# Layer 1's u and gate columns in pairs: seven half-size products for eight, on an x that is normalised before it is split

## The chip, the cores and the metric

The kernel runs on one core of a Trainium2 chip. The metric is the time of one execution in device microseconds; times shown are medians of runs, and the traces come from one profiled execution.

## The reference, cut to what matters

1,024 prompt rows and 64 sample rows (1,088 tokens, width 1,024) pass through two layers. The second one is the odd layer:

```
def _odd_layer(x, g_norm, w_in, ln_g, ln_b, w_s, b_s, w_out):
    z = _rmsnorm(x, g_norm) @ w_in                      # w_in: 1024 x 6144
    uv = jax.nn.gelu(z[..., :2 * D_C]); gate = z[..., 2 * D_C:]
    u = uv[..., :D_C]; v = _layernorm(uv[..., D_C:], ln_g, ln_b)
    # per head of 256 columns: causal 128x128 mixing of v inside each chunk of 128 rows
    y = (u * mix * jax.nn.silu(gate)) @ w_out
    return x + y, v[:, start:]
```

## The kernel before

Everything is float32 in exactness: each operand is split into a high part (type fp32r) and a low part (what is left), and a product is three matmuls, high x high, high x low, low x high, accumulated in one PSUM buffer. ScalarE copies the high part, VectorE subtracts to get the low one (`split`, L125 and the helper line L92; VectorE's operations made through helpers all bear the line L92, so its groups are told apart by their tiles).

x is held transposed, eight tiles of 128 features by 1,088 tokens, high and low. A unit (`unit`, `unit_w`, L460 to L468) makes 128 output columns for all tokens: three token pieces of 368, 352 and 368 columns (`PIECES`), and for each, eight depth tiles of three matmuls. Weights come by `wload` (512 KB each into two buffers `wr`) and `wsplit` (three buffers each of `wh`, `wl`, or a pair of the big pool for the roomy kinds); `wget` keeps two more split ahead.

The stages of the second half of the program: the fourth part of the first layer's output projection (unit after unit, each adds into x1, takes the square for the norm, and splits x1 times the norm's gain into `xh`, `xl`); `token_wide` for v (four groups of 512 columns, token rows as the stationary side, L545 to L556, evacuated through gelu with the row's norm factor `rc`, L1189, and statistics, L1190); then eight heads of 256 columns. In a head, two units give u and two give the gate, each evacuated from PSUM by a VectorE product with `rb`, the norm factor spread over partitions (L1163 to L1165); `prepare` normalises the head's v and transposes the mixing matrix; `mixed` applies it (L1274, L1279); y is split and stored to DRAM, except four of sixteen tiles that stay in SBUF for the first part of the last projection. `out_part` then adds four parts of depth 512, with operands fetched from DRAM during the part before.

The norm's per-row factors come from 18 one-column matmuls:

```
    for t in range(9):
        n = rows(t)
        mm(mp[0:n, t:t + 1], s2[:, t * P:t * P + n], one1[:, 0:1], start=True, stop=True)
```

The first layer is issued in an order written out by hand. From the fourth part of its projection on, only SyncE's queue (the loads) keeps the order of the program text; on the other engines a planner takes, of what it holds to be ready, the instruction that stands first in the text. SBUF tiles come from pools of fixed size, `ft` with 31 buffers being the large one; a tile waits until an older one has been read for the last time. PSUM has four buffers for units (`ps_mm`) and four for the rest.

Of the kernel before, what the change touches and what calls it, by code (L numbers as in the profile page):

```python
# [15 lines left out]
P = 128  # L16
D = 1024
# [4 lines left out]
T = NPR + NS  # L22
KD = D // P
# [12 lines left out]
def kernel(  # L36
# [91 lines left out]
    def wload(spec):  # L128
        kind, w2d, rws, c0 = spec
        shape = {"u": [P, 8, P], "h": [P, 4, 256], "q": [P, 2, 512], "qf": [P, 2, 512]}[kind]  # L130
# [3 lines left out]
        return raw, shape, kind == "qf"  # L134
# [37 lines left out]
    for part in (2, 3, 0, 1):  # L172
        for mg in range(4):
            plan_h(wo0, mg * 256, 4 * part, 1)
    for g in range(4):
        for q in range(4):
            wspecs.append(("q" if q % 2 == 0 else "qf", w1, 2 * q, 2048 + 512 * g))
    for h in range(8):
        for d in range(2):
            plan_u(w1, (2 * h + d) * P)  # L180
            plan_u(w1, 4096 + (2 * h + d) * P)
    PARTS1 = ([8, 9, 10, 11], [0, 1, 2, 3], [4, 5, 6, 7], [12, 13, 14, 15])
    for ks in PARTS1[:3]:
        for mg in range(4):
            plan_h(wo1, mg * 256, ks[0], 1)
# [156 lines left out]
    mcaus = cst.tile([P, P], I32, name="mcaus")  # L342
# [4 lines left out]
    bm4 = cst.tile([96, 4], F32, name="bm4")  # L347
# [4 lines left out]
    msamp = cst.tile([NS, NS], I32, name="msamp")  # L352
    mblk = cst.tile([NS, NSB], I32, name="mblk")
    scm = cst.tile([P, 512 + NS], F32, name="scm")
# [27 lines left out]
    cwt = cst.tile([P, CW, KD], F32, name="cwt")  # L382
# [4 lines left out]
    lbt = cst.tile([P, 4, KD], F32, name="lbt")  # L387
# [145 lines left out]
    def token_wide(ah, al, tail, evac):  # L533
# [5 lines left out]

        for t in range(8):  # L540
# [8 lines left out]
        ps = ps_mm("ps")  # L549
        for k in range(KD):  # L550
            wh, wl = w(k)
            if k > 0:
                mm(ps[0:NS, :], tail[:, k - 1, 0:NS], w(k - 1)[1], start=False, stop=False)
            if k == KD - 1:
                mm(ps[0:NS, :], tail[:, k, 0:NS], wl, start=False, stop=False)
            mm(ps, tail[:, k, :], wh, start=(k == 0), stop=(k == KD - 1))  # L556
        tl = th("tl", [NS, 512])
        act(out=tl, in_=ps[NS:P, :], func=AF.Copy)
        tt_op(out=tl, in0=ps[0:NS, :], in1=tl, op=ALU.add)
        evac(8, NS, tl)  # L560
# [573 lines left out]
    x1_d = dscr("x1_d", KD)  # L1134
    xh, xl = [], []
    s2 = None
    for mg in range(4):
        (wh, wl), = wget()
        for s in range(2):
            m = 2 * mg + s  # L1140
            ms = slice(s * P, (s + 1) * P)
            xm = x1[m]
            unit_w([(wh[:, k, ms], wl[:, k, ms]) for k in range(4)], bh, bl, accum(x1)(m))
            hi, lo = ft(f"gh{m}", F32R), ft(f"gl{m}", F32R)
            act(out=hi, in_=xm, func=AF.Copy, scale=col(o_nc, m))
            stt(out=lo, in0=xm, scalar=col(o_nc, m), in1=hi.bitcast(F32), op0=ALU.mult, op1=ALU.subtract)
            sq = ft("sq")
            act(out=sq, in_=xm, func=AF.Square)
            if s2 is None:
                s2 = sq  # L1150
            else:
                tt_op(out=s2, in0=s2, in1=sq, op=ALU.add)
# [245 lines left out]
```

## Time and profile before

| | |
|---|---|
| median of 3 runs | 1824.42 us (1821.47 to 1824.86) |
| the profiled execution | 1825.03 us, span 1823.2 us |
| TensorE, VectorE, ScalarE busy in the span | 1803.2, 1126.8, 682.8 us |
| mean granted TensorE clock | 0.998 of 2.4 GHz |
| moved to and from DRAM | 196.4 MB, 108 GB/s |

The span runs from the first to the last instruction; the execution's own time is 1.8 us longer. TensorE's busy time is a union of overlapping matmuls. A granted clock of 1.00 is 2.4 GHz, 0.50 is 1.2 GHz.

### The profile page before, as it was taken

The page shows a single profiled execution, that of the slowest core. Times are in us where ns is not written, and L with a number is a line of the kernel's source. Part 1 is how long each engine was busy: PE and PEld are TensorE (multiplying, and loading weights), DVE is VectorE, ACT ScalarE, POOL GpSimd, SP SyncE. Part 2 cuts the span into 40 slices and gives each one's busy share as a digit, 9 for nine tenths or more (in the row PEclk, how much of TensorE's full clock was granted, in tenths as well). Part 3 has the DMA queues.
Part 4 walks back from the last instruction along what each step waited for, and adds up shares of the span by engine and source line. Part 5 has one row for each costly group of instructions (what it writes and reads, how often), then busy time and mean ns, then how long its engine had stood idle before and what let it go on. Part 6 is the DMA issues. An engine that isn't in the chain of part 4 may idle for free.

```text
span 1823.2 us, 27162 instructions
## 1 busy us (share of the span) xinstructions
PE 1803.2 (99%) x11360; PEld 1742.8 (96%) x11360; DVE 1126.8 (62%) x1801; ACT 682.8 (37%) x1100; POOL 18.0 (1%) x50
## 2 busy tenths in 40 slices
PE   7999999999999999999999999999999999999998
PEld 6999999999999999999999888899999999999996
DVE  6468779878887878847776342244555454543434
ACT  5234442545255544645324232232323233320124
POOL 0000000000000000000000000000000000000000
PEclk9999999999999999999999999999999999999999
DMA  5112122213122212388423222334443221374501
GB/s 165 49 39 83 51 100 60 97 51 109 57 79 63 84 49 96 109 283 287 163 96 123 103 95 85 106 96 133 133 128 90 91 73 59 98 292 155 179 24 75
DMA packets 178650, 196.44 MB, mean 108 GB/s; under 512 B 7560, under 2 KB 151376, under 8 KB 178512
## 3 DMA queue, kind: packets, MB, share of 16 engines
q1 hardware_dynamic: 153256, 139.00, 24.0%
q10 hardware_dynamic: 25272, 55.71, 8.0%
q8 instruction: 89, 1.46, 0.3%
q14 instruction: 33, 0.27, 0.0%
HBM read 138.98 MB, written 56.42 MB: 107 GB/s over the span
## 4 chain that ended last, share of the span: by engine, by line
PE 98%; DVE 1%; ACT 1%; DMA 0%; issue 0%; ACTq 0%; SPq 0%; DVEq 0%
PE ps L466 23%; PE ps L468 23%; PE ps L467 23%; PE ps L547 3%; PE ps L545 3%; PE ps L546 3%; PE ps L504 2%; PE ps L505 2%; PE ps L506 2%; PE mp L1274 2%; PE ps L1354 1%; PE ps L1352 1%; PE ps L1353 1%; PE dp L777 1%; PE op L797 1%; PE op L857 1%
## 5 line engine op out<-in xcount | busy, mean ns | idle before, releaser
L466 PE MATMUL ps<-xh,wh 128*128 128x368 f32 (+1 forms) x1080 | 356.7, 330 | 0.0
L468 PE MATMUL ps<-xh,wl 128*128 128x368 f32 (+1 forms) x1080 | 352.8, 327 | 0.0
L467 PE MATMUL ps<-xl,wh 128*128 128x368 f32 (+1 forms) x1080 | 352.7, 327 | 0.0
L92 DVE SCALAR_TENSOR_TENSOR y<-ab,cwt,y 128x1024 f32<-128x1024 f32 x240 | 306.7, 1278 | 0.2
L125 ACT ACTIVATE wh<-wr 128x1024 fp32r<-128x1024 f32 x124 | 130.7, 1054 | 346.4 <-PE ps L467 248.1
L466 PE MATMUL ps<-gh,wh 128*128 128x368 f32 (+1 forms) x768 | 252.8, 329 | 0.0
L468 PE MATMUL ps<-gh,wl 128*128 128x368 f32 (+1 forms) x768 | 251.4, 327 | 0.0
L467 PE MATMUL ps<-gl,wh 128*128 128x368 f32 (+1 forms) x768 | 250.8, 327 | 0.0
L92 DVE TENSOR_TENSOR wl<-wr,wh 128x1024 fp32r<-128x1024 f32 x124 | 151.4, 1222 | 150.4 <-ACT wh L125 149.2
L466 PEld LDWEIGHTS ps<-xh,wh 128*128 128x128 f32 x1080 | 202.7, 188 | 1.3
L467 PEld LDWEIGHTS ps<-xl,wh 128*128 128x128 f32 x1080 | 202.8, 188 | 0.3
L468 PEld LDWEIGHTS ps<-xh,wl 128*128 128x128 f32 x1080 | 202.7, 188 | 0.0
L92 DVE TENSOR_TENSOR x<-ps,x 128x368 f32<-128x368 f32 x168 | 88.4, 533 | 115.4 <-PE ps L468 112.8
L466 PEld LDWEIGHTS ps<-gh,wh 128*128 128x128 f32 x768 | 144.2, 188 | 0.3
L467 PEld LDWEIGHTS ps<-gl,wh 128*128 128x128 f32 x768 | 144.2, 188 | 0.0
L468 PEld LDWEIGHTS ps<-gh,wl 128*128 128x128 f32 x768 | 144.2, 188 | 0.0
L466 PE MATMUL ps<-oh,wh 128*128 128x368 f32 (+1 forms) x384 | 127.6, 332 | 0.0
L468 PE MATMUL ps<-oh,wl 128*128 128x368 f32 (+1 forms) x384 | 125.5, 327 | 0.0
L467 PE MATMUL ps<-ol,wh 128*128 128x368 f32 (+1 forms) x384 | 125.4, 327 | 0.0
L92 DVE TENSOR_TENSOR g<-ps,rb 128x368 f32<-128x368 f32 (+1 forms) x48 | 25.7, 535 | 121.1 <-PE ps L468 121.1
L1190 DVE BATCH_NORM_STATS2 bst<-vq 128x6 f32<-128x512 f32 x32 | 22.0, 693 | 120.0 <-ACT vq L1189 120.0
L504 PE MATMUL ps<-wh,xh 128*128 128x256 f32 x256 | 72.9, 285 | 0.0
(328 smaller groups left out, 3402.5 us busy)
## 6 DMA issues: line engine op xcount, KB each, us to landing
wr<-in_w_in_ab_dram SPq DMA_DIRECT2D x56, 512.0 KB
wr<-in_w_in_c_dram SPq DMA_DIRECT2D x48, 512.0 KB
yr<-y_d SPq DMA_DIRECT2D x16, 544.0 KB
wr<-in_w_out_ab_dram SPq DMA_DIRECT2D x16, 512.0 KB
v_d<-vq ACTq DMA_DIRECT2D x16, 512.0 KB
wr<-in_w_out_c_dram SPq DMA_DIRECT2D x16, 512.0 KB
yh_d<-yh ACTq DMA_DIRECT2D x12, 544.0 KB
yl_d<-yl ACTq DMA_DIRECT2D x12, 544.0 KB
```

The lines of the kernel that those rows point to most:

```text
L92: return f(**kw)
L125: act(out=hi, in_=src, func=AF.Copy)
L466: mm(ps[:, 0:cn], wh, ah[k][:, cs], start=(k == 0), stop=False)
L467: mm(ps[:, 0:cn], wh, al[k][:, cs], start=False, stop=False)
L468: mm(ps[:, 0:cn], wl, ah[k][:, cs], start=False, stop=(k == n_k - 1))
L504: mm(ps[:, 0:256], ah[k][:, ts], wh, start=(k == 0), stop=False)
L505: mm(ps[:, 0:256], ah[k][:, ts], wl, start=False, stop=False)
L506: mm(ps[:, 0:256], al[k][:, ts], wh, start=False, stop=(k == KD - 1))
L545: mm(ps, ah[k][:, ts], wh, start=(k == 0), stop=False)
L546: mm(ps, ah[k][:, ts], wl, start=False, stop=False)
L547: mm(ps, al[k][:, ts], wh, start=False, stop=(k == KD - 1))
L1274: mm(mp[:, b * P:(b + 1) * P], vr[4 * g + b][:, ds_], wsT, start=True, stop=True)
```

## The change

- The four units of a head become two pairs: the two u units (256 columns), then the two gate units. Seen as a 2 x 2 block matrix (x halved by depth and by tokens, the weights by depth and by columns), a pair takes seven products of half depth (four tiles), half columns (128) and half tokens (544, in two pieces of 272) where plain multiplication takes eight. The blocks of sums and differences of x (`halves`) are made once, in the v part; those of the weights (`s_prep`) for each pair. Each product is added from PSUM into one or two of the four output quarters.
- x1's norm is applied to x before the split (`normed`), piece by piece; the output projection's last part runs pieces outside, units inside. The products with `rb` and the factors `rc` go, and with them the one-column matmuls.
- The nine normalisations of v per head move from VectorE to ScalarE. `mixed` multiplies u in place. All sixteen y tiles go to DRAM, in half tiles; the last projection takes them in order, its first part reloaded too.
- The small pools of the first layer are closed and new ones opened; the last v group does its sample rows first.

The diff, cut to its core:

```diff
+HT = T // 2
...
+            wspecs.append(("hf" if part == 1 and mg == 3 else "h", wo0, 4 * part, mg * 256))
     for g in range(4):
         for q in range(4):
...
+            kind = (("q", "q", "q", "qf"), ("qf", "qf", "q", "q"), ("q", "qf", "q", "qf"), ("q", "qf", "q", "q"))[g][q]
+            wspecs.append((kind, w1, 2 * q, 2048 + 512 * g))
+    PARTS1 = ([0, 1, 2, 3], [4, 5, 6, 7], [8, 9, 10, 11], [12, 13, 14, 15])
...
+    def token_wide(ah, al, tail, evac, tail_first):
...
+        if tail_first:
+            decode()
...
+    def cx(name, dt=F32):
+        return sp1.tile([P, HT], dt, tag="cx", bufs=4, name=name)
...
+    def tw(name, shape):
+        return sp1.tile(list(shape), F32, tag="tw", bufs=2, name=name)
...
+    xh = [ft(f"gh{m}", F32R) for m in range(KD)]
+    xl = [(ft if m < 5 else fu)(f"gl{m}", F32R) for m in range(KD)]
...
+    def normed(j, s2):
+        c0, cn = PIECES[j]
+        cs = slice(c0, c0 + cn)
+        mp = ps_ax("mp")
+        mm(mp[:, 0:cn], one1, s2, start=True, stop=True)
+        rb = cx("rb")[:, 0:cn]
+        act(out=rb, in_=mp[:, 0:cn], func=AF.Sqrt, scale=1.0 / D, bias=epsc)
+        nc.vector.reciprocal(out=rb, in_=rb)
+        for m in range(KD):
+            xn = cx("xn")[:, 0:cn]
+            stt(out=xn, in0=x1[m][:, cs], scalar=col(o_nc, m), in1=rb, op0=ALU.mult, op1=ALU.mult)
+            act(out=xh[m][:, cs], in_=xn, func=AF.Copy)
+            tt_op(out=xl[m][:, cs], in0=xn, in1=xh[m][:, cs].bitcast(F32), op=ALU.subtract)
+            yield
+    wq = wget(4)
+    for j, (c0, cn) in enumerate(PIECES):
+        cs = slice(c0, c0 + cn)
+        s2 = tw("s2", [P, HT])[:, 0:cn]
+        for m in range(KD):
+            wh, wl = wq[m // 2]
+            ms = slice(m % 2 * P, m % 2 * P + P)
+            ps = ps_mm("ps")
+            for k in range(4):
+                mm(ps[:, 0:cn], wh[:, k, ms], bh[k][:, cs], start=(k == 0), stop=False)
+                mm(ps[:, 0:cn], wh[:, k, ms], bl[k][:, cs], start=False, stop=False)
+                mm(ps[:, 0:cn], wl[:, k, ms], bh[k][:, cs], start=False, stop=(k == 3))
+            tt_op(out=x1[m][:, cs], in0=ps[:, 0:cn], in1=x1[m][:, cs], op=ALU.add)
+            store(out=x1_d[m][:, cs], in_=x1[m][:, cs])
+            if m == 0:
+                act(out=s2, in_=x1[m][:, cs], func=AF.Square)
             else:
+                sq = cx("sq")[:, 0:cn]
+                act(out=sq, in_=x1[m][:, cs], func=AF.Square)
                 tt_op(out=s2, in0=s2, in1=sq, op=ALU.add)
...
-
-    mp = ps_ax("mp")
-    for t in range(9):
-        n = rows(t)
-        mm(mp[0:n, t:t + 1], s2[:, t * P:t * P + n], one1[:, 0:1], start=True, stop=True)
...
+            aside()
+        side.append(normed(j, s2))
...
+    def halves(i):
+        def part(nm, k, cs):
+            t = cx(nm)
+            tt_op(out=t, in0=xh[k][:, cs].bitcast(F32), in1=xl[k][:, cs].bitcast(F32), op=ALU.add)
+            return t
+        def parted(r, t):
...
+            h, l = sums_h[r, i // 2][:, i % 2, :], sums_l[r, i // 2][:, i % 2, :]
+            act(out=h, in_=t, func=AF.Copy)
+            tt_op(out=l, in0=t, in1=h.bitcast(F32), op=ALU.subtract)
+        a21, s = part("a21", i, HI), part("a22", i + 4, HI)
+        yield
+        tt_op(out=s, in0=s, in1=a21, op=ALU.subtract)
+        parted(1, s)
+        yield
+        a11 = part("a11", i, LO)
+        tt_op(out=diff[i // 2][:, i % 2, :], in0=a11, in1=a21, op=ALU.subtract)
+        yield
+        stt(out=s, in0=s, scalar=-1.0, in1=a11, op0=ALU.mult, op1=ALU.subtract)
+        parted(2, s)
+        yield
+        a12 = part("a12", i + 4, LO)
+        stt(out=s, in0=s, scalar=-1.0, in1=a12, op0=ALU.mult, op1=ALU.subtract)
+        parted(3, s)
...
+    def s_load(c0):
+        ks = []
+        for q in range(2):
+            raw = wrp.tile([P, 4, 256], F32, tag="wr", name="wr")
+            load(out=raw, in_=w1[q * 512:(q + 1) * 512, c0:c0 + 256].rearrange("(k p) c -> p k c", p=P))
+            ks.append(raw)
+        return ks
+    def s_prep(ks, ops):
+        b11, b12 = ks[0][:, :, 0:P], ks[0][:, :, P:256]
+        b21, b22 = ks[1][:, :, 0:P], ks[1][:, :, P:256]
+        t41, t23 = tw("t41", [P, 2, 4, P]), tw("t23", [P, 2, 4, P])
+        tt_op(out=t41[:, 1], in0=b11, in1=b12, op=ALU.add)
+        tt_op(out=t23[:, 0], in0=t41[:, 1], in1=b22, op=ALU.add)
+        tt_op(out=t23[:, 1], in0=b22, in1=b12, op=ALU.add)
+        tt_op(out=t41[:, 0], in0=t23[:, 0], in1=b21, op=ALU.add)
+        for two in ((b11, t23[:, 0]), (b21, t23[:, 1]), (t41,), (b22,)):
+            wh = whp.tile([P, 2, 4, P], F32R, tag="wh", name="wh")
+            wl = whp.tile([P, 2, 4, P], F32R, tag="wl", name="wl")
+            if two[0] is t41:
+                split(wh, wl, t41)
+            else:
+                for e, src in enumerate(two):
+                    split(wh[:, e], wl[:, e], src)
+            ops.extend((wh[:, e], wl[:, e]) for e in range(1 if two[0] is b22 else 2))
+            yield
+    pairs = [c for h in range(8) for c in (256 * h, 4096 + 256 * h)]
+    sraw = []
...
+            aside(3 if g == 0 else 1)
+            if g == 0 and t == 4:
+                tl1.append(tails(xh, xl))
+            if t == 4 and g in (1, 2):
+                side.append(halves(g - 1))
+            if t == 0 and g == 3:
+                side.extend([halves(2), halves(3)])
+            if t == 2 and g == 3:
+                sraw.append(s_load(pairs[0]))
         if g == 0:
...
+            tl1 = []
+        token_wide(xh, xl, tl1, evac, g == 3)
+    aside(99)
+    tl1 = s2 = x1 = None
+    for i in range(4):
+        act(out=xh[i][:, HI], in_=diff[i // 2][:, i % 2, :], func=AF.Copy)
+        tt_op(out=xl[i][:, HI], in0=diff[i // 2][:, i % 2, :], in1=xh[i][:, HI].bitcast(F32), op=ALU.subtract)
+    diff = None
...
-            tsc(out=vr[t][0:n, :], in0=vr[t][0:n, :], scalar1=rv[0:n, t:t + 1], scalar2=nm[0:n, t:t + 1],
-                op0=ALU.mult, op1=ALU.add)
+            act(out=vr[t][0:n, :], in_=vr[t][0:n, :], func=AF.Identity, scale=rv[0:n, t:t + 1], bias=nm[0:n, t:t + 1])
...
+            us = u[:, g * 512:(g + 1) * 512]
+            tt_op(out=us, in0=us, in1=mx[:, 0:512], op=ALU.mult)
...
+    def a_(k0, cs):
+        return [(xh[k][:, cs], xl[k][:, cs]) for k in range(k0, k0 + 4)]
+    def s_(r):
+        return [(sums_h[r, i // 2][:, i % 2, :], sums_l[r, i // 2][:, i % 2, :]) for i in range(4)]
+    def pair_units(ops, d0, d1, func, after, ready):
+        xs = (a_(0, LO), s_(2), a_(4, LO), a_(0, HI), a_(4, HI), s_(1), s_(3))
+        for n, xk in enumerate(xs):
+            while len(ops) <= n:
+                after(-1)
+            wh, wl = ops[n]
+            for j in range(2):
+                ps = ps_mm("ps")[:, 0:HT // 2]
+                lo = slice(j * (HT // 2), (j + 1) * (HT // 2))
+                hi = slice(HT + lo.start, HT + lo.stop)
+                for k, (xhk, xlk) in enumerate(xk):
+                    mm(ps, wh[:, k], xhk[:, lo], start=(k == 0), stop=False)
+                    mm(ps, wh[:, k], xlk[:, lo], start=False, stop=False)
+                    mm(ps, wl[:, k], xhk[:, lo], start=False, stop=(k == 3))
+                if n == 0:
+                    act(out=d0[:, hi], in_=ps, func=AF.Copy)
+                for dst, src in (((), ((d1[:, lo], d0[:, hi]),), ((d0[:, lo], d0[:, hi]),), ((d1[:, hi], d1[:, lo]),),
+                                  ((d0[:, hi], d1[:, hi]),), ((d1[:, hi], d1[:, hi]), (d1[:, lo], d1[:, lo])),
+                                  ((d1[:, lo], d1[:, lo]),))[n]):
+                    tt_op(out=dst, in0=ps, in1=src, op=ALU.add)
+            if n in (2, 4, 5, 6):
+                d, cs = {2: (0, LO), 4: (0, HI), 5: (1, HI), 6: (1, LO)}[n]
+                dst = (d0, d1)[d][:, cs]
+                act(out=dst, in_=dst, func=func, scale=-1.0 if d else 1.0)
+                ready(d, cs)
+            after(n)
...
+    x2 = []
     hl = {0: head_load(0)}
...
+    nops = []
+    cur = s_prep(sraw.pop(), nops)
+    for _ in range(3):
+        next(cur)
...
+            def after(n, nops=nops, state=state, half=half, h=h, n_pair=n_pair):
+                if n in (-1, 1):
+                    turn_on(cur)
+                if n == 1 and n_pair + 1 < len(pairs):
+                    state["raw"] = s_load(pairs[n_pair + 1])
+                if n == 3 and state["raw"] is not None:
+                    state["gen"] = s_prep(state["raw"], nops)
+                if n in (3, 5, 6):
+                    turn_on(state["gen"])
+                if half == 0:
+                    if n == 0:
+                        next(prep)
+                    elif n == 2:
+                        got.append(next(prep))
+                elif n in (0, 2):
+                    mixed(h, n // 2, u[n // 2], *got[0])
+                    if n == 2 and h < 7:
+                        hl[h + 1] = head_load(h + 1)
+            def ready(d, cs, h=h, u=u):
+                if half == 0:
+                    return
+                k = 2 * h + d
+                tt_op(out=g_t[d][:, cs], in0=g_t[d][:, cs], in1=u[d][:, cs], op=ALU.mult)
+                hi = cx("yh", F32R)
+                act(out=hi, in_=g_t[d][:, cs], func=AF.Copy)
+                store(out=yh_d[k][:, cs], in_=hi.bitcast(F32))
+                lo = g_t[d][:, cs].bitcast(F32R)
+                tt_op(out=lo, in0=g_t[d][:, cs], in1=hi.bitcast(F32), op=ALU.subtract)
+                store(out=yl_d[k][:, cs], in_=g_t[d][:, cs])
+            if half == 0:
+                pair_units(ops, *u, func, after, ready)
             else:
...
+                g_t = [ft("g"), ft("g")]
+                pair_units(ops, *g_t, func, after, ready)
+            cur = state["gen"]
+    xh = xl = u = g_t = prep = sums_h = sums_l = None
+    x2 = [reload(x1_d[m], f"x2_{m}") for m in range(2)]
+    for ks in PARTS1[:3]:
+        for mg in range(4):
+            wspecs.append(("h", wo1, ks[0], mg * 256))
+    nxt[0] = ([], [])
+    for k in first:
+        nxt[0][0].append(reload(yh_d[k], "oh", F32R))
+        nxt[0][1].append(reload(yl_d[k], "ol", F32R))
```

## Rows read from the trace of the kernel before

**Rows 1.** The page's table of engines: busy us, share of the span, instructions.
```profile
PE 1803.2 (99%) x11360; PEld 1742.8 (96%) x11360; DVE 1126.8 (62%) x1801; ACT 682.8 (37%) x1100; POOL 18.0 (1%) x50
```

**Rows 2.** The chain that ended last, shares of the span by engine.
```profile
PE 98%; DVE 1%; ACT 1%; DMA 0%; issue 0%; ACTq 0%; SPq 0%; DVEq 0%
```

**Rows 3.** Windows: first layer, residual part, v part, one head; busy us by engine.
```profile
core 0: us, PE busy (x) PEld busy (x) DVE busy (x) ACT busy (x) POOL busy (x), PEclk, DMA share, GB/s
500.00:550.00 50.00, 50.00 (x324) 49.62 (x324) 44.35 (x65) 25.57 (x44) 0.00 (x0) 1.00 0.30 93
957.40:1005.54 48.14, 48.14 (x294) 48.14 (x293) 34.50 (x42) 20.31 (x19) 0.00 (x0) 1.00 0.39 136
1005.54:1200.00 194.46, 194.46 (x857) 158.69 (x857) 57.91 (x88) 54.01 (x67) 0.00 (x0) 0.99 0.27 94
1276.45:1328.50 52.05, 52.05 (x330) 51.90 (x331) 26.79 (x46) 16.22 (x16) 1.43 (x2) 1.00 0.37 117
```

**Rows 4.** Timeline of TensorE: start us, duration us, engine, line, operation.
```profile
95.07 0.28 PE L504 MATMUL ps<-wh,xh 128*128 128x256 f32 x1
...
102.63 0.28 PE L504 MATMUL ps<-wh,xh 128*128 128x256 f32 x1
...
104.85 0.33 PE L466 MATMUL ps<-xh,wh 128*128 128x368 f32 x1
...
108.86 0.32 PE L466 MATMUL ps<-xh,wh 128*128 128x352 f32 x1
...
112.70 0.33 PE L466 MATMUL ps<-xh,wh 128*128 128x368 f32 x1
```

**Rows 5.** Timeline of TensorE around the one-column matmuls.
```profile
1012.58 2.05 PE L1170 MATMUL mp<-oner,sq 128*128 128x1 f32 x18
1014.56 0.50 PE L545 MATMUL ps<-wh,gh 128*128 128x512 f32 x1
...
1015.81 0.61 PE L547 MATMUL ps<-wh,gl 128*128 128x512 f32 x1
...
1019.20 0.42 PE L547 MATMUL ps<-fwh,gl 128*128 128x512 f32 x1
```

**Rows 6.** Window just behind them; the columns are those of rows 3.
```profile
1016.00:1018.00 2.00, 2.00 (x6) 1.54 (x6) 0.16 (x3) 1.28 (x1) 0.00 (x0) 0.50 0.44 98
```

**Rows 7.** Groups of VectorE, one head, shapes apart: count | busy us, mean ns.
```profile
L92 DVE TENSOR_TENSOR wl<-wr,wh 128x1024 fp32r<-128x1024 f32 x4 | 4.9, 1220 | 0.8 <-ACT wh L125 0.8
L92 DVE SCALAR_TENSOR_TENSOR mx<-mp,prm,cb 128x512 f32<-128x512 f32 x4 | 2.9, 747 | 0.2 <-PE mp L1274 0.2
L92 DVE TENSOR_TENSOR g<-ps,rb 128x368 f32<-128x368 f32 x5 | 2.7, 541 | 13.6 <-PE ps L468 13.6
...
L92 DVE TENSOR_TENSOR u<-u,mx 128x1088 f32<-128x1088 f32 x2 | 2.6, 1288 | 0.0
```

**Rows 8.** Groups of ScalarE, same head.
```profile
L125 ACT ACTIVATE wh<-wr 128x1024 fp32r<-128x1024 f32 x5 | 5.3, 1059 | 31.7 <-PE ps L467 30.3 <-DMA wr<-in_w_in_c_dram 1.4
L1310 ACT ACT_TABLE_LOAD x2 | 2.6, 1283 | 0.0
...
L125 ACT ACTIVATE yh<-u 128x1088 fp32r<-128x1088 f32 x2 | 2.2, 1114 | 6.7 <-DVE u L92 6.7
```

**Rows 9.** Groups of VectorE, 1010 to 1225 us.
```profile
L1165 DVE RECIPROCAL rb<-rb 128x368 f32<-128x368 f32 x2 | 4.8, 2424 | 1.2 <-ACT rb L1164 1.2
```

**Rows 10.** Window of the last projection's reloads; columns of rows 3.
```profile
1630.00:1640.00 10.00, 10.00 (x63) 10.00 (x63) 3.81 (x6) 0.53 (x1) 0.00 (x0) 1.00 1.04 407
```

**Rows 11.** Timeline of SyncE's queue and of ScalarE: one weight load, its use.
```profile
1625.20 0.38 SPq L133 DMA_DIRECT2D wr<-in_w_out_c_dram  x1
...
1629.47 1.06 ACT L125 ACTIVATE wh<-wr 128x1024 fp32r<-128x1024 f32 x1 [7.04 <-DMA wr<-in_w_out_c_dram]
```

**Rows 12.** Timeline of VectorE: in brackets the idle time before, its releaser.
```profile
983.01 1.23 DVE L92 TENSOR_TENSOR wl<-wr,wh 128x1024 fp32r<-128x1024 f32 x1 [0.43 <-ACT wh L125]
...
1284.22 1.29 DVE L92 TENSOR_TENSOR yl<-u,yh 128x1088 fp32r<-128x1088 f32 x1 [1.18 <-ACT yh L125]
```

More of the change, by code (lines that the diff above doesn't have):

```diff
@@ L341 @@
     select(mcf, [[1, P]], 0, -1)
-    mcaus = cst.tile([P, P], I32, name="mcaus")
+    mcaus = cs0.tile([P, P], I32, name="mcaus")
     bmf = cst.tile([NS, NSB], F32, name="bmf")
@@ L346 @@
     select(bmf, [[NSS, NSB]], NSS - 1, -1)
-    bm4 = cst.tile([96, 4], F32, name="bm4")
+    bm4 = cs0.tile([96, 4], F32, name="bm4")
     msf = tb("msf", [NS, NSB, NSS])
@@ L538, in w, with decode @@
             return ws[k // 2][0][:, k % 2, :], ws[k // 2][1][:, k % 2, :]
+        def decode():
+            ps = ps_mm("ps")
+            for k in range(KD):
+                wh, wl = w(k)
+                if k > 0:
+                    mm(ps[0:NS, :], tail[0][:, k - 1, 0:NS], w(k - 1)[1], start=False, stop=False)
+                if k == KD - 1:
+                    mm(ps[0:NS, :], tail[0][:, k, 0:NS], wl, start=False, stop=False)
+                mm(ps, tail[0][:, k, :], wh, start=(k == 0), stop=(k == KD - 1))
+            tl = cx("tl")[0:NS, 0:512]
+            act(out=tl, in_=ps[NS:P, :], func=AF.Copy)
+            tt_op(out=tl, in0=ps[0:NS, :], in1=tl, op=ALU.add)
+            evac(8, NS, tl)
+        if tail_first:
+            decode()
         for t in range(8):
@@ L548, in token_wide @@
             evac(t, P, ps)
[L549 to L560, printed above, removed]
+        if not tail_first:
+            decode()
     def act_evac(dst, func):
@@ L1133 @@
     hand.close()
-    x1_d = dscr("x1_d", KD)
[L1135 to L1150, printed above, removed]
-            else:
+    only0.close()
@@ L1228, in head_load @@
         load(out=vs[0:NS, :], in_=vs_d[h // 2][:, hs])
-        gb = [smp.tile([P, 256], F32, tag="gb", name="gb") for _ in range(2)]
+        gb = [sp1.tile([P, 256], F32, tag="gb", name="gb") for _ in range(2)]
         load(out=gb[0], in_=ln_c_g[0:1, c0:c0 + 256].to_broadcast([P, 256]))
@@ new lines, in turn_on @@
+    def turn_on(gen):
+        if gen is not None:
+            next(gen, None)
+    x2 = []
+    hl = {0: head_load(0)}
+    nops = []
+    cur = s_prep(sraw.pop(), nops)
+    for _ in range(3):
+        next(cur)
+    first = PARTS1[0]
+    for h in range(8):
+        u = [ft("u") for _ in range(2)]
+        prep = prepare(h, *hl.pop(h))
+        got = []
+        for half, func in enumerate((AF.Gelu_apprx_tanh, AF.Silu)):
+            n_pair = 2 * h + half
+            ops, nops = nops, []
+            state = {"raw": None, "gen": None}
+            def after(n, nops=nops, state=state, half=half, h=h, n_pair=n_pair):
[29 more added lines that the diff above has]
+                pair_units(ops, *u, func, after, ready)
+            else:
+                g_t = [ft("g"), ft("g")]
+                pair_units(ops, *g_t, func, after, ready)
+            cur = state["gen"]
```

142 lines of the change are left out of this document (53 added, 89 removed).

## The prediction, made before the changed kernel ran

> **What bounds the kernel now.** I read the table of engines first: TensorE is busy 99% of the span, VectorE 62%, ScalarE 37% [rows 1]. A busy TensorE can still be waiting, so I read the chain of waits next: 98% of what sets the end is TensorE [rows 2]. Then the windows, one per stage [rows 3]: in the second layer's head loop (one head is 52.05 us, and the eight run from 1200.1 to 1616.5) TensorE never rests, VectorE works 26.79 us and ScalarE 16.22. Time is therefore bought only by giving TensorE fewer columns, and it is lost wherever another engine comes to hold it.
>
> What one matmul costs is the distance between starts; the duration printed beside it overlaps its neighbours. In [rows 4] the 63 matmuls of 256 columns from 95.07 to 102.63 are 0.1200 us apart; 24 of 368 columns take 108.86 - 104.85 = 4.01, 0.1671 each; 24 of 352 take 3.84, 0.1600. A column is thus about 0.42 ns, and some 13 ns come with every matmul whatever its width.
>
> **The pairs.** Removed per head: four units of 24 x (368 + 352 + 368) columns, 4 x (4.01 + 3.84 + 4.01) = 47.4 us. Added: two pairs of seven products, each 4 depth tiles x 3 terms x 2 halves of 272 columns, 336 matmuls. From the 256-column row, 0.1200 + 16 x 0.42 ns = 0.1267, so 42.6 us. TensorE is relieved of 4.9 us a head, 39.0 us over eight. The rest of a head (the mixing, its sums, a transpose) is 52.05 - 47.4 = 4.6 and stays, so a head becomes 47.2 if nothing holds TensorE. Columns fall by an eighth, the time by a tenth, since there are 336 matmuls where 288 stood.
>
> The Trainium skill (TensorE: Matmul & The Clock Gate, section Back-to-back issue gap) gives a warm matmul as its columns over 2.4 plus 2.5 ns. By that estimate the four units are 44.2 and the products 38.9, 42.6 us saved over eight heads; the rows here show about 13 ns beyond the columns, and the sum goes by them.
>
> **The norm.** The 18 one-column matmuls of L1170 go: 1014.56 - 1012.58 = 1.98 us [rows 5]. Just behind them eight matmuls of 512 columns take 1019.20 - 1015.81 = 3.39 us in place of 8 x 0.227 = 1.82 (the slope of rows 4), and the granted clock there is 0.50 [rows 6], the 1.2 GHz level; before it TensorE had done those thin matmuls. I count this 1.57 as regained too. The three sums over partitions that replace L1163 are the same matmuls. The residual part's 288 matmuls only change order. Gain: 39.0 + 2.0 + 1.6 = 42.5 us.
>
> **What VectorE is given in the pairs.** This is the price. From 1024 and 1088 elements (1220 and 1288 ns) an element is 1.06 ns [rows 7]: 512 elements 0.68, 544 0.71, 272 out of PSUM 0.541 - 0.102 = 0.44. Per head: 28 additions out of PSUM 12.3; eight weight sums 5.4; low halves of the weights, ten of 512 and two of 1024, 9.2; mixing 4 x 0.747 + 4 x 0.68 + small ones 0.95, 6.7; gate product and low half, eight of 544, 5.7; the rest of the preparation, by the same slope, 2.6. Together 42.0 in 47.2, 89%, where 26.8 in 52.05 stood. The first layer runs with 44.35 in 50 and TensorE full [rows 3], but much of that is convolution that nobody waits for soon; here a late addition holds a PSUM buffer. Four buffers of 12 x 0.1267 = 1.5 us each leave about 4.6 us from the end of a product to the end of its addition. The gate half is the tight one: 26 us of VectorE against 25 of TensorE; the u half, about 16 against 22, drains it. So I expect small stalls: 0.5 us a head, 4 us. Bounds: nothing, and the rival below.
>
> ScalarE: from 1.06 and 1.11 us for 1024 and 1088 elements and 1.28 for a table load [rows 8], per head weights 8.3, PSUM copies 1.6, eight activations 5.2, two table loads 2.6 (four now), nine normalisations taken over from VectorE 3.6, y copies 2.6: about 24 of 47. It is no bound, only a link.
>
> **Ahead of the pairs.** In pieces 1 and 2 of the residual part VectorE now does four operations of about 0.54 for each 12 matmuls of 2.0 us (addition, square sum, normalised x, low half): 2.16, and per piece one reciprocal of 2.42 [rows 9]. That is 19.7 a piece against 16.0 and 15.4; with two low weight halves 41.9 against 31.4, so VectorE is 10.5 us late when the v part starts. There the splits of the later weights stand behind this backlog in trace order. TensorE can fill some of it: three further row tiles can take their first four depth tiles, 3 x 12 x 0.227 = 8.2, since the planner takes what is ready. I take 4 us (ends 0 and 10.5), and 1.6 for one spell at the lower clock behind a stall (ends 0 and 3.2, two spells). The copies of x halves fit easily: about 32 us in the v part, where VectorE works 58 of 194 [rows 3]. At the start of the pairs the first weight split waits until the last row tile has read the buffer it gets: 1 us (0 to 2).
>
> **Behind the pairs.** Buffers ft: 8 high, 5 low, 12 sums, 2 v, 2 u, 2 g are all 31. Ten reloads now stand on SP's queue ahead of the first output weights, and they wait for buffers: four after the second product of the last pair (8 us into its 25), the rest after the fourth (16 us). Six of 0.557 MB at the 407 GB/s of [rows 10] take 8.2, the weights some 2 more, their split 1.06 + 0.43 + 1.22: about 29 to 30, so TensorE waits 4 us (ends 0 and 10). A 512 KB load now lands 4.3 us after its issue (1625.20 to 1629.47 [rows 11]), so the pairs' own loads, asked for 8 us into a pair and needed by 21, have cover; without it they would hold VectorE's weight sums first, then the additions behind them.
>
> **Sum.** 1825.0 (the profiled execution, 1.8 above its span) - 42.5 + 4 + 4 + 1.6 + 1 + 4 = 1797.1. That execution is 0.6 above the median of 1824.4, so 1796.
>
> **Rivals.** *All covered*: none of the stalls, 1825.0 - 42.5 - 0.6 = 1782. For it: TensorE is full at 89% VectorE in the first layer. Against: two handovers with 10 us of late work.
>
> *VectorE becomes the bound.* It waits about 0.43 us for ScalarE before a low weight half and 1.18 before a low y half of 1088 [rows 12], 0.65 if that shrinks with 544. Twelve and four such waits a head, none of them filled, make 42.0 + 5.2 + 2.6 = 49.8, or 51.9 with the full 1.18. That is 2.6 to 4.7 us over 47.2 a head, 21 to 38 in all, and with the 10.6 at the two ends 1813 to 1830. It turns a gain into a loss where a head passes 51.1. For it: VectorE runs in order and the gate half is over-full. Against: other work usually stands ready between.
>
> *Weight loads are the bound; slower.* The loads are busy 51.90 of 52.05 us with 331 of them [rows 3]. If 0.157 a load were their floor, 379 loads a head would take 59.6, 60 us more over the loop: about 1881. Against: the 256-column matmuls, each with its own load, come every 0.1200 [rows 4], which I take to refute it. The Trainium skill (Perfetto Trace Analysis, section Identifying the Most-Contended Engine) judges TensorE's headroom by the busy share of weight loads and would call this kernel bound by them; by that rule this rival holds, and the 0.1200 speaks against it.
>
> **Chances.** Forecast (1787 to 1806) 0.55; all covered 0.17; VectorE bound 0.24, of which 0.15 still clearly faster, 0.04 level, 0.05 slower; weight loads 0.04. A change under 0.2%, 3.6 us, can't be told from none. Faster 0.87, same 0.04, slower 0.09. The range 1781 to 1814 leaves out the weight loads, most of the VectorE case, and a little below.
>
> **What would show it.** Right: 272-column matmuls 0.127 us apart; a head of 47 to 48 us with VectorE near 42; no one-column matmuls near 1012; gaps of a few us on TensorE at the start of the v part and of the output part, each waiting for a low weight half. Wrong: TensorE idle in each head with additions out of PSUM as releaser; a spacing above 0.13; the granted clock at 0.5 inside the pairs; weight loads landing after 15 us.

## The result, and the profile after

The changed kernel takes 1792.43 us (median of 4 runs, 1792.15 to 1793.84) where the kernel before took 1824.42 beside it: a ratio of 0.983, with a 95% interval of [0.981, 0.985]. (One more execution of the kernel before fell into a slow state, 2228.28 us, and is left out of both.) The forecast was 1796, in a range of 1781 to 1814. The profiled execution took 1793.84, its span is 1792.1.

The page's table of engines and the chain that ended last, of the changed kernel:

```profile
PE 1762.7 (98%) x11726; PEld 1701.5 (95%) x11726; DVE 1254.4 (70%) x2147; ACT 753.3 (42%) x1342; POOL 18.7 (1%) x50
...
PE 92%; DVE 4%; DMA 2%; ACT 1%; issue 0%; SPq 0%; POOL 0%; ACTq 0%; DVEq 0%; POOLq 0%
```

TensorE still sets the end, but no longer all of it: its share of the chain was 98% [rows 2]. VectorE works 128 us more than in [rows 1]. The windows of the changed kernel, in the stages of [rows 3] (residual part, v part, eight heads, a gap, the last projection) and then one head; the columns are those of rows 3. Below them stand the eight heads of the kernel before:

```profile
958.00:1007.68 49.68, 48.88 (x293) 48.01 (x293) 37.38 (x66) 22.04 (x39) 0.00 (x0) 1.00 0.33 108
1007.68:1197.59 189.91, 189.91 (x835) 154.76 (x835) 96.48 (x165) 59.71 (x93) 0.00 (x0) 1.00 0.27 95
1197.59:1577.08 379.49, 376.14 (x3017) 374.12 (x3015) 296.56 (x607) 192.24 (x318) 11.65 (x15) 1.00 0.40 134
1577.08:1582.53 5.45, 0.16 (x3) 0.00 (x1) 1.82 (x4) 2.22 (x4) 0.00 (x0) 0.95 0.99 370
1582.53:1792.10 209.57, 202.56 (x1152) 191.64 (x1152) 88.40 (x152) 47.60 (x89) 0.00 (x0) 0.98 0.39 142
...
1271.17:1318.44 47.27, 46.99 (x379) 46.75 (x379) 37.31 (x76) 24.21 (x40) 1.79 (x2) 1.00 0.39 129
```

```profile
1200.09:1616.37 416.28, 416.28 (x2634) 415.15 (x2632) 212.18 (x363) 132.43 (x126) 10.71 (x14) 1.00 0.34 106
```

| stage | before, us | after, us | difference |
|---|---|---|---|
| up to the v part | 1005.54 | 1007.68 | +2.14 |
| v part | 194.55 | 189.91 | -4.64 |
| eight heads | 416.28 | 379.49 | -36.79 |
| TensorE waits for the first output weights | 0 | 5.45 | +5.45 |
| last projection | 206.83 | 209.57 | +2.74 |
| span | 1823.2 | 1792.1 | -31.1 |

Two of the three sums over partitions now stand ahead of the mark between the first two stages, so these are read together: -2.5. The heads bring the gain, and some 8 us of it, over a fifth, are lost behind them. From mark to mark a head is 47.23 to 47.51 us, 47.3 in the mean, where it was 52.05. The distance of two product matmuls, from TensorE's timeline (start, duration):

```profile
1206.45 0.29 PE L1420 MATMUL ps<-gh,wh 128*128 128x272 f32 x1
...
1214.71 0.29 PE L1420 MATMUL ps<-sh,wh 128*128 128x272 f32 x1
```

66 intervals in 8.26 us are 0.1252 each. TensorE's waits in the changed kernel (us in total, times, the longest), those that the change brought:

```profile
PE ps L465 <- ACT wh L129: 5.3, 1, 5.3
...
PE ps L1420 <- DVE g L96: 2.2, 7, 0.5
...
PE pst L1367 <- POOL wsT L335: 1.1, 1, 1.1
...
PE ps L560 <- DVE x L96: 0.8, 1, 0.8
```

The largest is the gap at 1577. The chain of waits through it (start, us, what), and TensorE's timeline behind it:

```profile
1572.24 9.10 DMA wr<-in_w_out_c_dram
...
1581.42 1.06 ACT wh L129
```

```profile
1576.95 0.29 PE L1422 MATMUL ps<-sh,wl 128*128 128x272 f32 x1
1582.53 0.67 PE L465 MATMUL ps<-oh,wh 128*128 128x368 f32 x1 [5.29 <-ACT wh L129]
...
1584.57 0.51 PE L466 MATMUL ps<-ol,wh 128*128 128x368 f32 x1
...
1586.41 0.51 PE L466 MATMUL ps<-ol,wh 128*128 128x368 f32 x1
...
1588.78 0.33 PE L467 MATMUL ps<-oh,wl 128*128 128x352 f32 x1
```

```profile
1583.00:1588.70 5.70, 5.70 (x20) 5.55 (x20) 3.14 (x4) 1.76 (x3) 0.00 (x0) 0.50 0.61 202
```

The weights are asked for at 1572.24 only and land 9.1 us later; ScalarE copies their high half, and by then TensorE has idled 5.3 us. Behind the idle time six intervals from 1584.57 to 1586.41 are 0.307 us each where the same matmul takes 0.167 [rows 4]: the granted clock is 0.50, the 1.2 GHz level, until 1588.78. That is the +2.74 of the last stage.

VectorE's groups of one head (count, busy us, mean ns, idle before), beside [rows 7]:

```profile
L96 DVE TENSOR_TENSOR u<-ps,u 128x272 f32<-128x272 f32 x14 | 5.8, 436 | 3.2 <-PE ps L1422 3.0
...
L96 DVE TENSOR_TENSOR wl<-wr,wh 128x512 fp32r<-128x512 f32 x6 | 4.1, 686 | 0.2
...
L96 DVE TENSOR_TENSOR g<-g,u 128x544 f32<-128x544 f32 x4 | 2.9, 718 | 0.0
```

The single durations are as forecast (436 for 440 ns, 686 for 680, 718 for 710), and count times mean over all groups of this view gives 42.1 us, the 42.0 that was forecast. Yet the window shows VectorE busy for 37.31.

### The profile page after: what moved, and what is told of

It reads as the page before. It is cut to its first block, busy times and chain, and to the rows that moved or that the text cites. A ratio compares the mean times of both kernels' runs of the same rounds, so it can differ in the third digit from the quotient of the medians.

```text
span 1792.1 us, 28730 instructions
## 1 busy us (share of the span) xinstructions
PE 1762.7 (98%) x11726; PEld 1701.5 (95%) x11726; DVE 1254.4 (70%) x2147; ACT 753.3 (42%) x1342; POOL 18.7 (1%) x50
## 4 chain that ended last, share of the span: by engine, by line
PE 92%; DVE 4%; DMA 2%; ACT 1%; issue 0%; SPq 0%; POOL 0%; ACTq 0%; DVEq 0%; POOLq 0%
PE ps L465 15%; PE ps L467 15%; PE ps L466 15%; PE ps L1420 5%; PE ps L1421 5%; PE ps L1422 5%; PE ps L560 3%; PE ps L562 3%; PE ps L561 3%; PE ps L503 2%; PE ps L505 2%; PE ps L504 2%; DMA wr<-in_w_in_c_dram 1%; PE ps L1535 1%; PE ps L1533 1%; PE ps L1534 1%
## 5 line engine op out<-in xcount | busy, mean ns | idle before, releaser
L96 DVE TENSOR_TENSOR wl<-wr,wh 128x1024 fp32r<-128x1024 f32 (+1 forms) x141 | 146.4, 1039 | 148.1 <-ACT wh L129 146.7
L129 ACT ACTIVATE wh<-wr 128x1024 fp32r<-128x1024 f32 (+1 forms) x141 | 128.0, 909 | 226.5 <-PE ps L466 81.1
L96 DVE TENSOR_TENSOR x<-ps,x 128x368 f32<-128x368 f32 (+1 forms) x168 | 88.3, 532 | 113.9 <-PE ps L467 105.3
L1420 PE MATMUL ps<-gh,wh 128*128 128x272 f32 x512 | 148.5, 290 | 0.0
L1422 PE MATMUL ps<-gh,wl 128*128 128x272 f32 x512 | 147.7, 288 | 0.0
L1421 PE MATMUL ps<-gl,wh 128*128 128x272 f32 x512 | 147.5, 288 | 0.0
L1420 PE MATMUL ps<-sh,wh 128*128 128x272 f32 x384 | 111.9, 292 | 2.2 <-DVE g L96 2.2
L1421 PE MATMUL ps<-sl,wh 128*128 128x272 f32 x384 | 110.6, 288 | 0.0
L1422 PE MATMUL ps<-sh,wl 128*128 128x272 f32 x384 | 110.6, 288 | 0.0
L465 PEld LDWEIGHTS ps<-oh,wh 128*128 128x128 f32 x480 | 91.1, 190 | 5.9 <-ACT wh L129 5.5
```

The source lines that it names most:

```text
L96: return f(**kw)
L129: act(out=hi, in_=src, func=AF.Copy)
L465: mm(ps[:, 0:cn], wh, ah[k][:, cs], start=(k == 0), stop=False)
L1420: mm(ps, wh[:, k], xhk[:, lo], start=(k == 0), stop=False)
L1421: mm(ps, wh[:, k], xlk[:, lo], start=False, stop=False)
L1422: mm(ps, wl[:, k], xhk[:, lo], start=False, stop=(k == 3))
```

## The experiments

The theory: TensorE's matmul count sets the heads; VectorE's added work is hidden, since VectorE is busy 37.3 of 47.3 us; the 8.2 us at the end come from the order on SyncE's queue. The rivals: VectorE's sums already cost time in the heads, weight loads are close to a bound, the end is due to bytes or buffers. All times below stand against 1792.4. The runs with 24 or 48 additions, narrow products, one-column matmuls and the normalisation on VectorE are one execution each; they stand against the profiled execution, 1793.84, and a difference of 1 or 2 us in them is no more than executions of one kernel differ by (1792.15 to 1793.84 here).

### Output weights ahead of the reloads

```
-    x2 = [reload(x1_d[m], f"x2_{m}") for m in range(2)]
...
+    sooner = [wload(wspecs.popleft()) for _ in range(2)]
     for k in first:
...
+    x2 = [reload(x1_d[m], f"x2_{m}") for m in range(2)]
+    wready.extend(wsplit(rw) for rw in sooner)
```

> Edit: after the last pair, SyncE's queue gets the two first loads of output weights ahead of the reloads of the split activations, and the two reloads of x1 last. Theory A, the order on the queue makes the gap of 5.45 us between the last product (1577.08) and the first output matmul (1582.53), and the idle engine brings the slower matmuls behind it (about 19 of .306 us rather than .167, 2.6 us): the gap shrinks to under 1.5 us, the clock near 1580 stays at 1.0, and the time falls by 5 to 8 us, to 1785 to 1788. Rival B, the gap comes from the bytes of the ten reloads themselves or from buffers that come free with the last pair's end: the gap stays within 1.5 us of 5.45 and the time within 2 us of 1792.4.

Measured: 1786.66 us (1786.23 to 1788.12), 0.981 [0.979, 0.982] of the kernel before; 5.8 less than the changed kernel, and 7.6 less between the two profiled executions. SyncE's queue in the changed kernel, and then in this one (start, us of issue):

```profile
1559.33 0.81 SPq L572 DMA_DIRECT2D x<-x_d  x2
...
1569.34 0.32 SPq L572 DMA_DIRECT2D ol<-yl_d  x1
1572.24 2.80 SPq L138 DMA_DIRECT2D wr<-in_w_out_c_dram  x2
```

```profile
1546.22 15.83 SPq L138 DMA_DIRECT2D wr<-in_w_out_c_dram  x2
...
1576.03 1.67 SPq L572 DMA_DIRECT2D x<-x_d  x2
```

And its windows around the end of the heads:

```profile
1575.00:1580.00 5.00, 4.59 (x33) 4.28 (x32) 4.70 (x9) 2.30 (x4) 0.00 (x0) 1.00 1.02 400
1580.00:1585.00 5.00, 5.00 (x33) 5.00 (x31) 2.15 (x4) 0.66 (x1) 0.00 (x0) 1.00 0.99 331
```

The same ten reloads move, at 400 GB/s around the end of the heads, and the gap is 0.41 us; the clock stays at 1.00. The queue's order made both losses; the rival of bytes and buffers falls as their main cause. The 0.41 us that are left are a wait for a reload. The edit also puts the two reloads of x1 last; what that alone gives was not tried.

### Eight plain products in the same frame

```
-        xs = (a_(0, LO), s_(2), a_(4, LO), a_(0, HI), a_(4, HI), s_(1), s_(3))
+        xs = (a_(0, LO), a_(0, HI)) * 2 + (a_(4, LO), a_(4, HI)) * 2
...
+                if n < 4:
+                    act(out=dst, in_=ps, func=AF.Copy)
+                else:
+                    tt_op(out=dst, in0=ps, in1=dst, op=ALU.add)
```

> Edit: in the same frame (half-depth, 272-column tiles, weights split pair by pair), each pair takes eight plain products in place of the seven, with no sums of weights or of x used; the split halves' sums are still computed ahead of the pairs, and the result is that of plain products. Theory A, TensorE's product count sets the pairs' time and what VectorE does beside it is hidden: 48 more matmuls in a head at .1252 us add 6.0 us, a head takes 53.3, and the time is 1792 + 48 = 1840 (range 1835 to 1845), above the kernel before, whose head took 52.05 with larger tiles. Rival B, VectorE's sums (weights and outputs) already bound the heads: a head with eight plain products has fewer VectorE instructions and takes under 52 us, the time under 1830.

Measured: 1832.57 us (1831.78 to 1833.02), 1.0054 [1.004, 1.007] of the kernel before. One head's window:

```profile
1277.99:1330.78 52.79, 52.79 (x427) 52.79 (x427) 25.62 (x52) 25.29 (x48) 0.60 (x2) 1.00 0.35 116
```

A head takes 52.79 with TensorE never idle, though VectorE has 11.7 us less to do. The frame alone (narrower matmuls, all y through DRAM, the same end) makes the kernel 0.5% slower than before; the gain is the dropped eighth product, 5.5 us a head, against 6.0 expected (48 x 0.1252): the seven-product head loses some 0.5 us to waits that this one has not. The total came out 7 below what was expected; 8 x 0.5 of it is there, and 2 at the end, where this kernel waits 3.2 us for output weights instead of 5.3; the spell at the lower clock behind that wait is shorter too (3.4 us at 0.50, from 1623.0).

### One-column matmuls put back

```
+            if t == 6 and g == 1:
...
+                for c in range(9):
+                    mm(mp1[:, c:c + 1], dst[:, c * 32:c * 32 + P], one1[:, 0:1], start=True, stop=True)
```

> Edit: eighteen instructions' worth of one-column matmuls (nine fp32 products with one output column each, as the statistics of a row tile had before) are put back at one place of the v part of layer 1, at the last row tile of the second weight group; their result goes nowhere. Theory A, these instructions cost what the trace of before shows around them, 1.98 us, and a spell of the lower clock follows, 1.57 us: the v part takes 189.9 + 2.0 + 1.6 = 193.4, with a stretch at clock .5 to .9 behind the place. Rival B, the lower clock in the trace of before had another cause (the wait on VectorE at that point): 191.9, and the clock stays 1.0.

TensorE's timeline at the place:

```profile
1095.04 2.11 PE L1300 MATMUL mp<-oner,vq 128*128 128x1 f32 x18
1097.02 0.48 PE L561 MATMUL ps<-fwl,gh 128*128 128x512 f32 x1
```

1.98 us again, as in [rows 5], or 0.110 for each of 18 instructions with one column; the granted clock stayed at 1.00 in every window from 1085 to 1110. The time, 1797.15, is 3.3 more: 1.98 here, 1.9 in the heads, where TensorE waits 4.1 us for additions out of PSUM instead of 2.2, and 0.6 less at the end, where it waits 4.7 us instead of 5.3. The same group at twelve places of the v part, `t in (0, 4, 6)` in each weight group:

> Edit: the group of nine one-column fp32 products (eighteen instructions), which cost 1.98 us and brought no fall of the clock at one place of the v part, is put at twelve places there, three in each of the four weight groups; its results go nowhere. Theory A, the fall of the clock in the trace of before (4 us at .50) was not the one-column products' doing: 12 x 1.98 = 23.8 more in the v part, the clock at 1.0 all through. Rival B, they bring it in some places: each of these shows a stretch at .5 and 1.6 us more, with half of them some 33 in all.

1825.75 us, 31.9 more in the span. Twelve groups are 23.8, and two of them waited 0.38 and 1.55 us for their input. Behind three of the twelve the clock fell. Two of these (at 1050.68 and 1105.78) had no idle time before them; the third (at 1183.59) is the group that had waited 1.55 us, so there the idle time may have had a part. Windows around the first and the third, 1.00 before:

```profile
1050.00:1055.00 5.00, 5.00 (x30) 4.33 (x29) 0.69 (x1) 0.75 (x2) 0.00 (x0) 0.89 0.01 3
1055.00:1060.00 5.00, 5.00 (x18) 3.81 (x18) 0.23 (x1) 0.60 (x1) 0.00 (x0) 0.77 0.00 0
...
1185.00:1190.00 5.00, 5.00 (x20) 4.09 (x21) 4.44 (x8) 1.39 (x3) 0.00 (x0) 0.70 0.04 11
```

Each fall costs about 1.7 us (of the first, 0.11 x 5 + 0.23 x 5). So neither theory holds as put: a group of thin matmuls can bring the lower clock, and mostly doesn't; the v part of the changed kernel, without such groups, stays at 1.00. The runs don't show what tells the three from the nine.

### VectorE's load: v's normalisation back, then idle instructions

```
-            act(out=vr[t][0:n, :], in_=vr[t][0:n, :], func=AF.Identity, scale=rv[0:n, t:t + 1], bias=nm[0:n, t:t + 1])
+            tsc(out=vr[t][0:n, :], in0=vr[t][0:n, :], scalar1=rv[0:n, t:t + 1], scalar2=nm[0:n, t:t + 1],
+                op0=ALU.mult, op1=ALU.add)
```

> Edit: the nine instructions of a head that normalise v go from ScalarE back to VectorE, nine of about .41 us. Theory A, VectorE is occupied for 37.3 of the 47.25 us of a head, since its instructions overlap: with 3 more us it stands near 40.5, and the head stays at 47.2 to 47.6, the time within 3 us of 1792.4. Rival B, occupancy is the sum of the printed durations (41.3 in a head): 45 of 47.25, where waits can no longer be absorbed: 0.5 to 2 us more in a head, 4 to 16 us in all.

1794.98 us, 1.1 more, which is within what executions differ by. Three heads are 47.29 to 47.44, and one is 47.89; one of them:

```profile
1272.19:1319.50 47.31, 47.01 (x379) 46.77 (x379) 40.03 (x85) 19.75 (x31) 1.81 (x2) 1.00 0.39 129
```

VectorE takes the nine instructions as 2.7 us of busy time, and the head stays where it was. Moving them to ScalarE was not needed. Then idle instructions were added, two behind each product but the first of a pair, and in a later run four:

```
+            if n > 0:
+                for _ in range(2):
+                    tt_op(out=scr, in0=dst, in1=scr, op=ALU.max)
```

> Edit: each product but the first is followed by two further VectorE instructions of its 272 columns (maximum with a tile of scratch, result used for nothing), 24 in each unit pair or 48 in a head. Each is printed at about .43 us and starts some .36 us after the one before it where they follow one another. Theory A, what counts is the start-to-start time (busy time of the windows, 37.3 of 47.25 us now): 37.3 + 48 x .36 = 54.6 in a head, over TensorE's 47; the head becomes 54 to 56, 7 to 9 us more, 55 to 70 us in all, 1850 to 1862. Rival B, the printed durations count (41.3 now): 41.3 + 48 x .43 = 61.9, the time 1905 to 1915. Rival C, VectorE's load is hidden by another cause than its slack: no change.

This expectation counts the edit wrongly: two behind each of six products in two pairs are 24 in a head, not 48. With 24 the theory's own numbers are 37.3 + 24 x 0.36 = 45.9, still under 47.25, so no change; the rival's are 41.3 + 24 x 0.43 = 51.6, some 35 us more. Measured: 1798.95 us, 5.1 more, near the theory and far from the rival.

```profile
1284.15:1332.00 47.85, 47.26 (x379) 46.82 (x379) 45.09 (x102) 23.99 (x40) 0.60 (x2) 1.00 0.40 127
```

VectorE is busy 45.1 us of this head, 94%, and the head is 0.6 us longer (the heads are 47.6 to 48.9). In all, TensorE waited for additions out of PSUM ten times, 5.7 us, and never over 1.2 at once (seven times, 2.2 us, in the changed kernel).

> Edit: 48 idle VectorE instructions of 272 columns in a head instead of the 24 of an earlier run, which added 7.8 us of busy time to VectorE in a head (.325 each) and .6 us to the head. Theory A, VectorE bounds a head once its busy time passes TensorE's 47: 37.3 + 48 x .325 = 52.9 in a head, so a head takes 53 to 54.5 and the time is 1840 to 1852. Rival B, the instructions never bound it, and the cost goes on at .6 us for each 24: 48.5 in a head, 1804.

1852.48 us, at the upper end of the theory's 1840 to 1852. Two heads, from one transpose of the mixing weights to the next:

```profile
1242.13:1296.60 54.47, 49.82 (x380) 48.59 (x378) 51.25 (x121) 22.35 (x37) 1.32 (x2) 0.97 0.32 106
1296.60:1351.80 55.20, 49.12 (x380) 48.52 (x378) 52.89 (x125) 24.39 (x41) 1.58 (x2) 0.97 0.34 110
```

Now VectorE sets the pace, at 94 to 96% busy over heads of 55 us; the granted clock is 0.97 in the mean of each, so a spell at the lower level takes a part of the time. TensorE's waits in this run that were under 2.3 us in the changed kernel:

```profile
PE pst L1367 <- POOL wsT L335: 21.5, 8, 3.2
PE ps L1420 <- DVE g L96: 13.3, 8, 2.1
...
PE ps L1420 <- DVE u L96: 6.5, 9, 2.0
```

19.8 us wait for additions out of PSUM; another 21.5 for GpSimd's selection of the mixing weights, which ScalarE's copy releases. In the first of the two heads that copy stands directly behind a weight copy that had waited 0.65 us for VectorE; the other heads were not followed. The rival that the prediction feared is real, and it begins some 8 us of VectorE a head further on than the changed kernel stands.

### Narrower products

```
+                for o in (0, HT // 4):
+                    po, lq = ps[:, o:o + HT // 4], slice(lo.start + o, lo.start + o + HT // 4)
...
+                        mm(po, wh[:, k], xhk[:, lq], start=(k == 0), stop=False)
```

> Edit: each product matmul of 272 columns is issued as two of 136 columns into the halves of the same tile, with the same weights: 672 weight loads and 672 matmuls in a head in place of 336. Theory A, a matmul's start-to-start time is its columns at 2.4 GHz and some 13 ns: .0695 us each, 46.7 in place of 42.1, a head takes about 51.9, the time 1792 + 37 = 1829. Rival B, the weight load is the bound, or close to it (the weight loads' busy share of a head is 99% at .1252 us): .12 to .125 us each, 82 in place of 42 in a head, the time 1792 + 320 = 2110.

2045.91 us; a head is 79.59. TensorE's timeline of it:

```profile
1299.77 0.27 PE L1424 MATMUL ps<-gh,wl 128*128 128x136 f32 x1
...
1303.90 0.28 PE L1422 MATMUL ps<-gh,wh 128*128 128x136 f32 x1
```

37 intervals in 4.13 us, 0.112 each, where columns and 13 ns would give 0.070. The theory's price fell: half the width takes 0.013 us off a product, not 0.055. The rival's 0.12 was nearer, and still too high. A one-column matmul costs nearly the same, 0.110. Yet 0.11 is not the floor of every matmul, as the mixing of the changed kernel shows:

```profile
1271.89 1.06 PE L1386 MATMUL mp<-wsT,vb 128*128 128x128 f32 x8
1272.79 0.33 PE L1394 MATMUL mp<-wsb,vs 128*128 128x64 f32 x2
1272.93 0.37 PE L1420 MATMUL ps<-sh,wh 128*128 128x272 f32 x1
```

Instructions of 128 columns start 0.11 us apart, the two of 64 columns 0.07. Whether the weight load or something else in a matmul sets these prices was not tried: each product here brings its own load.

### Both waits removed

The first head's mixing weights are transposed ahead of the first pair, beside the order of the first experiment:

```
+    prep0 = prepare(0, *hl.pop(0))
+    next(prep0)
     for h in range(8):
...
-        prep = prepare(h, *hl.pop(h))
+        prep = prepare(h, *hl.pop(h)) if h else prep0
```

> Edit: the output weights' first loads ahead of the reloads on SyncE's queue, as in the run before that took 1786.66 us, and the first head's transposed table of spatial weights, on which TensorE waits 1.13 us for GpSimd at 1202.01, is made once ahead of the first pair. Theory A, both waits are on TensorE's path and independent: 1785.5 us (1784 to 1787), no wait of a product or a sum for GpSimd at the start of the first head. Rival B, another instruction of the first pair (the recip and offset of v's statistics on VectorE, the first weight sums) is as late, and the wait goes there: 1786.7.

1787.75 us (1786.27 to 1789.75), 0.981 [0.979, 0.982] of the kernel before, the same as the first experiment within what can be measured. TensorE's timeline at the start of the first head:

```profile
1200.87 0.38 PE L1368 MATMUL pst<-wsT,oner 128*128 128x128 f32 x2
...
1203.41 0.40 PE L1421 MATMUL ps<-sh,wh 128*128 128x272 f32 x1 [2.03 <-ACT wh L129]
```

The wait for GpSimd is gone, and the next product waits 2.03 us for its weights' high half: the rival was right. In the changed kernel that half was ready at 1202.47, only 0.46 us after the wait for GpSimd ended at 1202.01, so there was next to nothing to gain. The first experiment's kernel stays the simplest of the two that are equally fast.

## Why the prediction was right, point by point

- **Columns and count: right.** 336 matmuls of 0.1252 us (forecast 0.1267), a head of 47.3 (forecast 47.2). The eight-product kernel shows that this is where the gain is made. The head agrees better than its parts: cheaper products gave 0.5 us a head more than forecast, and the waits in the heads, named next, took it back. And the prediction's 13 ns with every matmul "whatever its width" do not hold for narrow ones, as the products of 136 columns show.
- **VectorE in the heads: the size of the stalls right, the load too high, the cause only in part the one named.** The prediction summed printed durations to 42.0 us, 89%. The window has 37.31, 79%: consecutive VectorE instructions overlap in the trace, as here, where one of 0.69 us is followed 0.60 after its start (timeline of VectorE, changed kernel):

```profile
1293.55 0.69 DVE L96 TENSOR_TENSOR wl<-wr,wh 128x512 fp32r<-128x512 f32 x1
1294.15 0.69 DVE L96 TENSOR_TENSOR wl<-t,wh 128x512 fp32r<-128x512 f32 x1
```

  The stalls were put at 0.5 a head and 4 in all. The profile counts 2.2 us of idle time in seven places, one in each head but the last, always in the gate half, as forecast. Measured from start to start, as the eight-product head shows, a place costs some 0.5 us, so 4 in all is about right. But the gate half is not over-full (26 us of VectorE against 25 were forecast): VectorE is busy 18.75 of its 25.20 us. What the chain of waits shows there, then TensorE's wait at its end, and VectorE's windows (gate half, and from the landing on):

```profile
1277.56 3.62 DMA wr<-in_w_in_c_dram
1281.20 1.29 DVE t L96 x2
```

```profile
1287.62 0.39 PE L1420 MATMUL ps<-sh,wh 128*128 128x272 f32 x1 [0.28 <-DVE g L96]
```

```profile
1268.00:1293.20 25.20, 24.92 (x203) 24.68 (x202) 18.75 (x38) 14.00 (x24) 1.48 (x1) 1.00 0.39 125
1281.20:1290.50 9.30, 9.02 (x72) 8.78 (x72) 9.30 (x19) 6.51 (x13) 1.48 (x1) 1.00 0.74 235
```

  VectorE waits 1.50 us for the next pair's weights, which were asked for at 1277.56; from 1281.20 it works without a rest through weight sums, gate products and mixing, and the addition out of PSUM that TensorE needs comes behind them. That is what the prediction feared of a load without cover, and took to be covered. No run moved these loads, so that an earlier load would remove the stall is not shown.

  The break-even of the rival was put at 51.1 us a head; the run with 24 more instructions stays below it (some 48), and the one with 48 more passes it (55).
- **Start of the pairs: 1 forecast, 1.1 of idle time measured, of another cause.** Not the weight split, but GpSimd's selection of the mixing weights; when that is moved, the split does come late. That the number agrees is luck.
- **Ahead of the pairs: 4 forecast, about 1 measured.** VectorE was late as forecast (10.5 us): the normalised x of the middle piece (352 columns) is still being split at 1014.81, 7 us after the v part began, and the last piece's only at 1033.57. TensorE filled the wait with the first depth tiles of further row tiles, which the prediction had counted as possible, and lost 0.8 us in one place, not to a low weight half but to an addition into x1; with its 1.98 for the one-column matmuls and 1.57 for the clock, the first two stages would gain 3.5 without a loss, and they gain 2.5.
- **The clock: 1.57 gained as forecast; 1.6 forecast as lost, 2.74 measured, at another place.** The fall at 1016 is gone. The spell that was forecast behind a stall ahead of the pairs did not come (1.00 in the v part); one came behind the gap at the end. That the thin matmuls caused the fall at 1016 is likely and not shown: the same group brought one in 3 of 13 places, once with idle time before it.
- **Behind the pairs: mechanism right, size too small.** 4 forecast, 5.45 measured: the loads of the output weights stood behind ten reloads that waited for buffers, were issued only at 1572.24, and took 9.1 us beside the reloads, where the prediction gave the weights some 2. TensorE waited for their high half, not for the low one that the prediction named as the sign.
- **Weight loads as the bound: rejected, and nearer than the prediction took it.** They are busy 99% of a head (46.75 of 47.27), and a product still comes each 0.1252, with 379 loads a head where 331 stood; but narrower products came no closer than 0.112. The Trainium skill (Perfetto Trace Analysis, section Identifying the Most-Contended Engine) takes the busy share of weight loads, beside the share of peak arithmetic, as the measure of TensorE's headroom. By that share the heads had none before (51.90 of 52.05 us) and have next to none now, and they still became 4.8 us shorter. In the run with products of 136 columns the share is 100% and the time does stand at 0.112 a product; the changed kernel's 0.1252 is 12% above that.

The losses, from start to start, come to 1.0 ahead of the pairs, about 1.4 at the start of the first head, about 3.9 in seven gate halves, 5.45 for the gap and 2.74 for the clock: 14.5 us, where 14.6 were forecast. (In the heads these are the distances from a transpose of the mixing weights to TensorE's next instruction, 1.40 us in the first head and 0.51 to 0.78 at the seven stalls, less the 0.03 that the same distance takes in the eight-product run.) That the sums agree is partly luck: 3 too much ahead of the pairs stand against 1.5 and 1.1 too little at the end. What the forecast missed is the gain without losses: 31.1 + 14.5 = 45.6 us where it had 42.5. The spacing of the products accounts for that: 8 x 336 x 0.0015 = 4.0 us.

## What to carry to other kernels

Replacing one of eight products pays as long as the matmuls do not become so narrow that their columns no longer set their price: here 272 columns cost 0.125 us each, 136 columns 0.112, and at half the width a head took 79.6 us in place of 47.3. Sum VectorE's load from starts, or take the window's busy time, not from printed durations, and ask what its work waits for: here, by the chain of waits, the stalls followed a load and not a half that was full; VectorE could be busy 45 us of a head of 48 before more than half a microsecond of it showed. Where one stage hands over to the next, look at what stands ahead of the first load on its queue: two loads moved past ten gave 5.8 us, a fifth as much as the whole change.

## What the runs showed of the hardware that was not expected

- Products of 136 columns, mixing instructions of 128 and single-column ones all start 0.11 us apart, two mixing instructions of 64 columns 0.07; 256 columns take 0.120, 272 take 0.125.
- Behind 3 of 13 like groups of thin matmuls, one of them with 1.55 us of idle time before it, the clock fell, for a loss of about 1.7 us each; idle time of 5.3 us on TensorE brought it as well, and 0.41 us did not.
- VectorE took the 24 further instructions of a head, printed at 0.43 us each, as 7.8 us of busy time (45.09 - 37.31), 0.32 each.
